# A two-part transformer block in fp32: the MLP's mean squares, the residual's scale and the final norm's root computed in another way

## The chip, the cores and the metric

The kernel runs on one core of one Trainium2 chip. The metric is the time of one execution in device microseconds (us); lower is better. Weights, inputs and the result lie in the chip's HBM.

## What is computed

A sequence of 256 tokens of width 1024 goes through two blocks. The first has two layers, each a mixer (convolution with attention, then a gated linear recurrence) and an MLP of width 4096; the second is an attention block with modulation. Cut to what the change touches:

```python
def rmsnorm(x, g):
    xf = x.astype(jnp.float32)
    y = xf * lax.rsqrt(jnp.mean(xf * xf, axis=-1, keepdims=True) + EPS)
    return (y * g.astype(jnp.float32)).astype(x.dtype)

def first_block(x, ...):
    for layer in range(DEPTH):                     # DEPTH = 2
        h = rmsnorm(x, mix_norm[layer])
        ...
        x = x + y
        x = x + sq_relu_mlp(rmsnorm(x, mlp_norm[layer]), w_up[layer], w_down[layer])
    return rmsnorm(x, final_norm)

def second_block(x, c, ctx, ...):
    ...
    y = (jax.nn.sigmoid(ga) * ya + jax.nn.sigmoid(gb) * yb) @ w_out[i]
    x = x + gate * y
    return rmsnorm_2(x, final_g)                   # the same formula
```

`sq_relu_mlp(h, up, down)` is the square of relu(h @ up), times down. As the square scales with the square of h, the MLP's norm can be put behind it: its output is multiplied by 1 / (mean square + eps), which the code calls R2, with no root.

## The kernel before

**Layout.** Activations stand transposed: 128 channels of a group on the partitions, 8 groups, 256 tokens along the free axis (`x` is 128 x 8 x 256). Every fp32 weight is split into a rounded part and its residue (`wh`, `wl`), every activation too, and one product becomes three on TensorE (`mm3`, lines 358 to 362).

**Weights.** 240 blocks of 128x1024 come in a fixed order through `fetch` (line 300): a DMA on SyncE's queue into one of four `raw` buffers, then ScalarE's copy to `wh` (line 307) and a subtraction to `wl` on VectorE or GpSimd (line 310; the table `POLICY` says which). Six buffers of each kind, ten from the first MLP to the fourth step of the second, hold what is ready; `unit` keeps up to six blocks prepared ahead. A load waits until the residue of the block four earlier has been taken from its buffer, and all loads of SyncE stand in one queue.

**The MLP** (`mlp`, lines 939 to 985). Sixteen steps p: two blocks of `up` give 256 hidden channels (`mm`), ScalarE takes relu and square (lines 955, 956), GpSimd the exact square (957), VectorE the residue (`mal`, line 407). From p = 2 on, two blocks of `down` per step are summed into four PSUM tiles `acc`. The last four rows of `down` and the addition to the residual come in `proj_tail`, which needs R2 (line 835). At p = 4 `ssq` sums the squares of x over the channel groups (ScalarE, GpSimd); at p = 6 `csum` (line 424) sums over the partitions with two products of one column, tokens on the partitions, and VectorE adds eps and takes the reciprocal of 128x2 numbers (`rv`); at p = 8 `spread` turns these back with two products with the identity (line 442) and a ScalarE copy (448) into a 128x256 tile that holds the scale of each token on every partition.

**Beside the first MLP** the modulation of the second block is computed: 12 loads of 1 MB (`mw`, line 880, on SyncE's queue among the weight loads, two buffers) and 40 multiply-and-sum operations on VectorE (`mdump`, line 883), then a few small operations on their sums (`mod`, lines 926 to 935).

**The second block.** `b2_head` computes `r1`, the root of the first block's final norm, two numbers per partition. `b2_kv` makes keys and values, `b2_attn` the attention, `b2_out` the output projection: `oproj` and gates for four pairs p, then eight rows of `w_out` into PSUM. At p = 1 `b2_out` spreads `r1` (line 1461) and multiplies the residual by it (1463). The final norm: for each pair of channel groups b, VectorE adds the gated output to the residual (1492), ScalarE squares it (1493), `fold` adds the two squares of a pair (1484; GpSimd for b below 2, VectorE else); `scale` multiplies by the gain (1481). `stat` (1477) sums over channels with one-column products, five of them; `meaneps` (VectorE, 430), a power -0.5 on GpSimd (`rsq`, 435) and `across` (442) give the scale, with which the five output pieces are multiplied (1511) and stored.

The order of the instructions on each engine is set by a scheduler from the order of the code; `issue_after` holds an instruction back behind a named one.

## Time and profile before

| | us |
|---|---|
| median of three timed runs | 832.42 |
| lowest, highest | 828.91, 835.37 |
| the profiled execution | 829.35 |
| its span, first to last instruction | 827.5 |
| TensorE busy in the span | 790.3 |
| VectorE busy | 589.2 |
| ScalarE busy | 457.4 |
| GpSimd busy | 220.6 |

Engines in rows: PE is TensorE, PEld its weight loads, DVE VectorE, ACT ScalarE, POOL GpSimd, SP SyncE; a q behind a name is the engine's queue, which issues transfers. A row of the timeline has the start, the time until its last instruction ends, engine, line, operation, written tile, read tiles, form and count, and in brackets how long the engine stood idle before it and what ended that. Products on TensorE overlap: their lengths add up to more than the time they take, so the time of a group is read from the starts. An fp32 product that isn't split leaves two records.

### The profile page before, as it was taken

To read this page: it belongs to the slowest core of one execution; us is meant where nothing else is said; L and a number is where in the kernel's file an instruction comes from. 1 tells how busy PE (TensorE), PEld (TensorE's weight loads), DVE (VectorE), ACT (ScalarE), POOL (GpSimd) and SP (SyncE) were. 2 spreads that over 40 slices of the span, in tenths; PEclk is the share of its full clock that TensorE was granted. 3 is DMA by queue.
4 is the path that set the end of the run, shared out by engine and by line. 5 is a ranking of instruction groups with operands and counts; after the bars stand their busy time and mean duration, and the time that the engine had idled before them with its cause. 6 is when DMAs were issued, how large, how long until landed. Compare 5 with 4: busy or idle time off the path is not lost.

```text
span 827.5 us, 16152 instructions
## 1 busy us (share of the span) xinstructions
PE 790.3 (96%) x6476; PEld 757.8 (92%) x6476; DVE 589.2 (71%) x956; ACT 457.4 (55%) x722; POOL 220.6 (27%) x160
## 2 busy tenths in 40 slices
PE   6999899999999978798999999999999999999996
PEld 6997799999999978698999999999989988889996
DVE  6899659999997698898638445557634877566743
ACT  5578546544446625576636444545626587765433
POOL 4886634110111465500441101111000022220001
PEclk9999999999999999799999999999999999999998
DMA  7864357878878744318646566665234532554621
GB/s 237 305 204 128 102 179 240 336 269 301 289 275 280 250 120 136 112 49 303 222 126 202 185 183 201 191 194 177 85 126 142 165 104 101 179 166 166 204 78 51
DMA packets 41259, 152.32 MB, mean 184 GB/s; under 512 B 4576, under 2 KB 5088, under 8 KB 39008
## 3 DMA queue, kind: packets, MB, share of 16 engines
q1 hardware_dynamic: 40752, 149.19, 55.4%
q10 hardware_dynamic: 432, 2.10, 0.6%
q8 instruction: 51, 0.84, 0.4%
q14 instruction: 24, 0.20, 0.1%
HBM read 149.17 MB, written 2.10 MB: 183 GB/s over the span
## 4 chain that ended last, share of the span: by engine, by line
PE 74%; DVE 11%; ACT 5%; DMA 3%; issue 3%; POOL 2%; SPq 0%; POOLq 0%; DVEq 0%; ACTq 0%
PE mm L360 13%; PE mm L361 13%; PE mm L362 12%; PE acc L361 10%; PE acc L360 9%; PE acc L362 9%; DMA raw<-in_wst 3%; PE acc L1320 2%; PE acc L1348 2%; PE mm L1357 2%; DVE wl L310 2%; ACT wh L307 1%; DVE ysl L407 1%; POOL wl L310 1%; PE mm L442 1%
## 5 line engine op out<-in xcount | busy, mean ns | idle before, releaser
L307 ACT ACTIVATE wh<-raw 128x1024 fp32r<-128x1024 f32 (+1 forms) x198 | 207.1, 1049 | 185.6 <-PE mm L361 77.3
L310 DVE TENSOR_TENSOR wl<-raw,wh 128x1024 fp32r<-128x1024 f32 (+1 forms) x167 | 208.8, 1257 | 109.5 <-ACT wh L307 109.4
L361 PE MATMUL mm<-xsl,wh 128*128 128x256 f32 x824 | 229.7, 279 | 1.5 <-DVE xsl L847 1.5
L360 PE MATMUL mm<-xsh,wh 128*128 128x256 f32 x824 | 231.0, 280 | 0.0
L362 PE MATMUL mm<-xsh,wl 128*128 128x256 f32 x824 | 229.6, 279 | 0.0
L360 PEld LDWEIGHTS mm<-xsh,wh 128*128 128x128 f32 x824 | 156.0, 189 | 3.7 <-issue 3.3
L361 PEld LDWEIGHTS mm<-xsl,wh 128*128 128x128 f32 x824 | 156.0, 189 | 2.6 <-DVE xsl L847 2.1
L362 PEld LDWEIGHTS mm<-xsh,wl 128*128 128x128 f32 x824 | 155.6, 189 | 0.0
L957 POOL TENSOR_TENSOR ma<-mr 128x512 f32<-128x512 f32 x32 | 49.7, 1554 | 233.7 <-ACT mr L955 233.7
L361 PE MATMUL acc<-mal,wh 128*128 128x256 f32 x384 | 106.6, 278 | 0.7 <-DVE mal L407 0.7
L360 PE MATMUL acc<-mah,wh 128*128 128x256 f32 x384 | 106.7, 278 | 0.0
L362 PE MATMUL acc<-mah,wl 128*128 128x256 f32 x384 | 106.3, 277 | 0.0
L310 POOL TENSOR_TENSOR wl<-raw,wh 128x1024 fp32r<-128x1024 f32 x36 | 87.9, 2463 | 27.9 <-ACT wh L307 27.2
L361 PEld LDWEIGHTS acc<-mal,wh 128*128 128x128 f32 x384 | 72.4, 188 | 1.3 <-DVE mal L407 1.3
L362 PEld LDWEIGHTS acc<-mah,wl 128*128 128x128 f32 x384 | 72.1, 188 | 0.0
L360 PEld LDWEIGHTS acc<-mah,wh 128*128 128x128 f32 x384 | 72.1, 188 | 0.0
L307 ACT ACTIVATE wxh<-raw 128x1024 fp32r<-128x1024 f32 x35 | 36.6, 1056 | 34.7 <-DMA raw<-in_wst 27.0
L883 DVE CUSTOM_DVE_ANT_0 mdump<-mw,cv 128x1024 f32<-128x1024 f32 x40 | 51.0, 1274 | 3.4 <-DMA mw<-in_modw 3.1
L310 DVE TENSOR_TENSOR wxl<-raw,wxh 128x1024 fp32r<-128x1024 f32 x34 | 43.7, 1305 | 9.4 <-ACT wxh L307 9.4
L361 PE MATMUL mm<-xsl,wxh 128*128 128x256 f32 x168 | 47.5, 283 | 1.9 <-DVE xsl L847 1.9
L360 PE MATMUL mm<-xsh,wxh 128*128 128x256 f32 x168 | 47.6, 284 | 0.2 <-ACT xsh L841 0.2
L362 PE MATMUL mm<-xsh,wxl 128*128 128x256 f32 x168 | 47.2, 281 | 0.0
(374 smaller groups left out, 1765.1 us busy)
## 6 DMA issues: line engine op xcount, KB each, us to landing
raw<-in_wst SPq DMA_DIRECT2D x240, 512.0 KB, 4.1
mw<-in_modw SPq DMA_DIRECT2D x12, 1024.0 KB, 7.5
nb<-in_nab SPq DMA_DIRECT2D x16, 256.0 KB, 3.6
ab<-in_alibi ACTq DMA_DIRECT2D x1, 1536.0 KB, 7.8
x<-in_xT SPq DMA_DIRECT2D x4, 256.0 KB, 5.2
cv<-in_cvec SPq DMA_DIRECT2D x1, 1024.0 KB, 4.7
cx<-in_cT SPq DMA_DIRECT2D x1, 1024.0 KB, 6.5
xd<-x SPq DMA_DIRECT2D x1, 1024.0 KB, 4.4
```

Source lines behind the costliest of these rows:

```text
L307: nc.scalar.activation(wh, r, AF.Copy)
L310: (nc.vector if lo == "v" else nc.gpsimd).tensor_tensor(wl, r, wh.bitcast(F32), op=ALU.subtract)
L360: mm(out, w[0], x[0], start=start, stop=False, skip_group_check=True)
L361: mm(out, w[0], x[1], start=False, stop=False, skip_group_check=True)
L362: return mm(out, w[1], x[0], start=False, stop=stop, skip_group_check=True)
L407: self.nc.vector.tensor_tensor(l, src, h.bitcast(F32), op=ALU.subtract)
L442: self.lasts = self.nc.tensor.matmul(ps[:, j * 128:(j + 1) * 128], rc[:, j:j + 1].to_broadcast([128, 128]), self.ident, start=True, stop=True)
L883: V.tensor_tensor_reduce(d, w, cv[:, s * 1024:(s + 1) * 1024], 0.5, 0.0, op0=ALU.mult, op1=ALU.add, accum_out=self.mod[:, s * 24 + i:s * 2 ...
L957: G.tensor_tensor(a, r, r, op=ALU.mult)
L1320: PE.matmul(sc[i], Q[tag, h][a][:, qs], K[tag, h][b], start=a + b == 0, stop=a == 1)
L1348: PE.transpose(pt[:, i * 128:(i + 1) * 128], P[:, i * 128:(i + 1) * 128], self.ident)
L1357: PE.matmul(o[64 * hh:64 * hh + 64, :T], vt[:, i, h * 64:h * 64 + 64], PTs[tag, h][:, i], start=i == 0, stop=i == 3, skip_group_check=True)
```

## The change

In the MLP, at p = 6, one product takes the place of the two of `csum`: the 128x256 tile of squares is the moving operand and a 128x128 tile of ones the fixed one, so that the sum over partitions comes out on every partition at once, as a 128x256 tile. VectorE multiplies, adds eps and takes the reciprocal of all 256 columns. The spread at p = 8 is gone. A pad of 32 bytes in layer 0 stands where `rv` stood, so that later tiles keep their addresses. `r1` is spread at the end of `b2_kv` into the pool of the second block (its later tiles move by 1024 bytes), not in `b2_out`. In the final norm the folds of b = 0 and 1 are added on GpSimd, so that there are four statistics, not five; the root is taken by ScalarE, the reciprocal by VectorE; ScalarE's table for roots is loaded behind the last tanh; the scalings of b = 2 and 3 come behind the root.

```diff
@@ -968,11 +968,13 @@
             if p == 4:
                 parts = self.ssq(mp, x)
             if p == 6:
-                v = self.meaneps(self.csum(parts), D)
-                rv = self.t(self.cp, [128, 2], "rv")
-                V.reciprocal(rv, v)
-            if p == 8:
-                R2 = self.spread(mp, rv, "R2")
+                if l == 0:
+                    self.pad(self.cp, 32)
+                ms = self.ps()[:, :T]
+                PE.matmul(ms, self.ones, parts[0], start=True, stop=True)
+                R2 = self.t(mp, [128, T], "R2")
+                V.tensor_scalar(R2, ms, 1.0 / D, EPS, op0=ALU.mult, op1=ALU.add)
+                V.reciprocal(R2, R2)
             if p >= 2:
                 for k in (2 * p - 4, 2 * p - 3):
                     self.krow(acc, self.unit("down"), A.pop(k), k == 0, False)
@@ -1257,6 +1259,7 @@
                 V.scalar_tensor_tensor(cf[:, k], cf[:, k], self.p("gcq", k), RQ, op0=ALU.mult, op1=ALU.mult)
                 self.split(cf[:, k], cq[0][:, k], cq[1][:, k])
         zpair("za", 1, ep, cqn)
+        d["R1"] = self.spread(bp, d["r1"], "R1")
         d.update(kb=kb, vb=vb, krh=krh, krl=krl, ck=ck, wk=wk, va=va, bp=bp)
         q8 = self.t(self.cp, [128, 8, T], "hch")
         for i in range(2):
@@ -1389,7 +1392,7 @@
         def gdone(nm, p):
             def f(ps):
                 tg[nm, p] = self.t(bp, [128, 512], f"t{nm}", bufs=2)
-                S.activation(tg[nm, p], ps, AF.Tanh, scale=0.5)
+                self.lastt = S.activation(tg[nm, p], ps, AF.Tanh, scale=0.5)
             return f
 
         def gpair(nm, p):
@@ -1458,14 +1461,17 @@
             V.tensor_tensor(y, y, tg["gb", p], op=ALU.add)
             self.split(self.pair(y), ys[0][:, 2 * p:2 * p + 2], ys[1][:, 2 * p:2 * p + 2])
             if p == 1:
-                R1 = self.spread(op, d["r1"], "R1")
                 for k in range(8):
-                    V.scalar_tensor_tensor(x[:, k], x[:, k], self.p("fin", k), R1, op0=ALU.mult, op1=ALU.mult)
+                    V.scalar_tensor_tensor(x[:, k], x[:, k], self.p("fin", k), d["R1"], op0=ALU.mult, op1=ALU.mult)
         def orow(w, k, ms, end):
             for m in ms:
                 o = last[:, :T] if m == 7 else acc[m // 2][:, (m % 2) * T:(m % 2 + 1) * T]
                 c = slice(m * 128, m * 128 + 128)
                 self.mm3(o, (w[0][:, c], w[1][:, c]), yrow(k), k == 0 and (m % 2 == 0 or m == 7), end)
+        eps = self.t(op, [128, 1], "eps")
+        G.memset(eps, EPS)
+        with self.tc.issue_after(self.lastt.ins):
+            S.activation(self.warm, self.warm, AF.Sqrt)
         for k in range(6):
             orow(self.unit("wo2"), k, range(8), False)
         ws = [self.unit("wo2") for _ in range(2)]
@@ -1478,7 +1484,8 @@
                           stop=end, skip_group_check=True)
         def scale(b):
             for k in (2 * b, 2 * b + 1):
-                S.activation(x[:, k], x[:, k], AF.Copy, scale=self.p("fg2", k))
+                i = S.activation(x[:, k], x[:, k], AF.Copy, scale=self.p("fg2", k))
+            return i
 
         def fold(b):
             (G if b < 2 else V).tensor_tensor(sq[b][:, 0], sq[b][:, 0], sq[b][:, 1], op=ALU.add)
@@ -1498,14 +1505,20 @@
         with self.tc.issue_after(xi.ins):
             fold(2)
         with self.tc.issue_after(si.ins):
-            for b in range(1, 4):
-                scale(b)
+            sc = scale(1)
+        G.tensor_tensor(sq[0][:, 0], sq[0][:, 0], sq[1][:, 0], op=ALU.add)
         stat(sq[0][:, 0], True)
-        stat(sq[1][:, 0])
         stat(sq[3][:, 0])
         stat(sq[2][:, 0])
         stat(sq[3][:, 1], end=True)
-        RF = self.across(self.rsq(self.meaneps(st[:, :2], D)))
+        sd = self.t(op, [128, 2], "sd")
+        with self.tc.issue_after(sc.ins):
+            sd_ = S.activation(sd, st[:, :2], AF.Sqrt, scale=1.0 / D, bias=eps)
+        with self.tc.issue_after(sd_.ins):
+            scale(2)
+            scale(3)
+        V.reciprocal(sd, sd)
+        RF = self.across(sd)
         for i, (k0, k1) in enumerate(((0, 1), (1, 3), (3, 5), (5, 7), (7, 8))):
             xb = x[:, k0:k1]
             V.tensor_tensor(xb, xb, self.b2(RF, k1 - k0), op=ALU.mult)
```

What moves in the order. SyncE's queue in the first MLP, where `raw` are weight loads and `mw` modulation loads, before:

```order
L300 DMA raw_2814<-in_wst 128x1024
L880 DMA mw_3328<-in_modw 128x2048
L300 DMA raw_2846<-in_wst 128x1024
L300 DMA raw_2879<-in_wst 128x1024
L880 DMA mw_3402<-in_modw 128x2048
L300 DMA raw_2909<-in_wst 128x1024
L300 DMA raw_2951<-in_wst 128x1024
L880 DMA mw_3507<-in_modw 128x2048
L300 DMA raw_2983<-in_wst 128x1024
L300 DMA raw_3016<-in_wst 128x1024
L300 DMA raw_3048<-in_wst 128x1024
```

and now:

```order
L300 DMA raw_2808<-in_wst 128x1024
L300 DMA raw_2840<-in_wst 128x1024
L880 DMA mw_3322<-in_modw 128x2048
L300 DMA raw_2873<-in_wst 128x1024
L300 DMA raw_2903<-in_wst 128x1024
L880 DMA mw_3396<-in_modw 128x2048
L300 DMA raw_2945<-in_wst 128x1024
L300 DMA raw_2977<-in_wst 128x1024
L300 DMA raw_3010<-in_wst 128x1024
L880 DMA mw_3501<-in_modw 128x2048
L300 DMA raw_3042<-in_wst 128x1024
```

The numbers in the names differ by a few between the two programs (raw_2951 is now raw_2945); the last `mw` stands behind raw_3010, which was raw_3016, two weight loads further back, and the one before it one load further back.

VectorE in the same place, where `mdump` reads a modulation load, `wl` and `wxl` are weight residues and `mal` that of an MLP pair, before:

```order
L883 ISA mdump_3509,mod_1436<-mw_3507,cv_1433 128x1024
L883 ISA mod_1436 128x1
L310 TENSOR_TENSOR wxl_2954<-raw_2951,wxh_2953 128x1024
L883 ISA mdump_3541,mod_1436<-mw_3507,cv_1433 128x1024
L883 ISA mod_1436 128x1
L926 TENSOR_TENSOR mod_1436<-mod_1436,par_70 128x24
L932 SCALAR_TENSOR_TENSOR Ax_3726<-mod_1436,par_70 128x8
L935 TENSOR_SCALAR gate_3728<-mod_1436 128x8
L933 TENSOR_TENSOR Ax_3726<-Ax_3726,par_70 128x8
L310 TENSOR_TENSOR wxl_2986<-raw_2983,wxh_2985 128x1024
L310 TENSOR_TENSOR wxl_3019<-raw_3016,wxh_3018 128x1024
L310 TENSOR_TENSOR wxl_3051<-raw_3048,wxh_3050 128x1024
```

and now:

```order
L883 ISA mdump_3503,mod_1436<-mw_3501,cv_1433 128x1024
L883 ISA mod_1436 128x1
L310 TENSOR_TENSOR wxl_2980<-raw_2977,wxh_2979 128x1024
L883 ISA mdump_3535,mod_1436<-mw_3501,cv_1433 128x1024
L883 ISA mod_1436 128x1
L310 TENSOR_TENSOR wxl_3013<-raw_3010,wxh_3012 128x1024
L926 TENSOR_TENSOR mod_1436<-mod_1436,par_70 128x24
L932 SCALAR_TENSOR_TENSOR Ax_3720<-mod_1436,par_70 128x8
L935 TENSOR_SCALAR gate_3722<-mod_1436 128x8
L933 TENSOR_TENSOR Ax_3720<-Ax_3720,par_70 128x8
L310 TENSOR_TENSOR wxl_3045<-raw_3042,wxh_3044 128x1024
L407 TENSOR_TENSOR mal_2940<-ma_2938,mah_2939 128x512
```

Two weight residues that stood behind the small operations on the sums (wxl_2986 and wxl_3019, now 2980 and 3013) stand ahead of them, one between the two reductions and one behind the second; the residue that stood between the reductions is ahead of both.

TensorE at the end of the program, where csq_1503 to csq_1506 (now 1499 to 1502) are the squares of the four pairs, before:

```order
L362 MATMUL mm_9158<-kb_9152,wl_9781 128x256
L1477 MATMUL mm_9808<-ones_83,csq_1503_9809 128x1 x2
L1477 MATMUL mm_9808<-ones_83,csq_1504_9810 128x1 x2
L1477 MATMUL mm_9808<-ones_83,csq_1506_9812 128x1 x2
L1477 MATMUL mm_9808<-ones_83,csq_1505_9811 128x1 x2
L1477 MATMUL mm_9808<-ones_83,csq_1506_9812 128x1 x2
L442 MATMUL mm_9902<-ident_78,rc_9900 128x128 x2
```

and now:

```order
L362 MATMUL mm_9150<-kb_9144,wl_9771 128x256
L1483 MATMUL mm_9798<-ones_83,csq_1499_9799 128x1 x2
L1483 MATMUL mm_9798<-ones_83,csq_1502_9802 128x1 x2
L1483 MATMUL mm_9798<-ones_83,csq_1501_9801 128x1 x2
L1483 MATMUL mm_9798<-ones_83,csq_1502_9802 128x1 x2
L442 MATMUL mm_9890<-ident_78,sd_9883 128x128 x2
```

One statistic is gone, and what is spread is VectorE's `sd`, no longer GpSimd's `rc`; the first statistic reads a tile that GpSimd's added operation writes.

## Rows read from the trace of the kernel before

**Rows 1.** The page, busy time, share of the span and instructions of engines.

```profile
PE 790.3 (96%) x6476; PEld 757.8 (92%) x6476; DVE 589.2 (71%) x956; ACT 457.4 (55%) x722; POOL 220.6 (27%) x160
```

**Rows 2.** Windows: length, PE, PEld, DVE, ACT, POOL busy (instructions), clock, DMA, GB/s.

```profile
185.00:200.00 15.00, 15.00 (x131) 15.00 (x130) 14.93 (x22) 6.07 (x8) 3.07 (x2) 1.00 0.89 296
284.00:310.00 26.00, 20.85 (x177) 20.05 (x175) 23.11 (x27) 7.56 (x14) 15.48 (x9) 1.00 0.45 132
...
480.00:560.00 80.00, 80.00 (x708) 80.00 (x708) 41.14 (x38) 38.22 (x44) 11.18 (x7) 1.00 0.63 195
...
640.00:660.00 20.00, 19.97 (x160) 18.92 (x159) 17.51 (x29) 10.62 (x16) 0.71 (x1) 1.00 0.55 175
```

**Rows 3.** Timeline of TensorE: a layer-0 statistic, and that of the first MLP.

```profile
89.08 0.70 PE L780 MATMUL mm<-conv,on 128*128 128x256 f32 x2 [0.24 <-DVE conv L581]
89.62 0.72 PE L424 MATMUL mm<-ones,conv 128*128 128x1 f32 x6
...
175.46 0.50 PE L424 MATMUL mm<-ones,ssum 128*128 128x1 f32 x4
...
176.02 0.28 PE L361 MATMUL acc<-mal,wh 128*128 128x256 f32 x1
```

**Rows 4.** Timeline of TensorE at the spread in the output stage.

```profile
760.40 0.60 PE L442 MATMUL mm<-ident,r 128*128 128x128 f32 x4
...
760.96 0.28 PE L361 MATMUL mm<-xsl,wh 128*128 128x256 f32 x1
```

**Rows 5.** VectorE: the small reciprocal (timeline), and a 128x256 form (shortest/median/longest, ns).

```profile
189.59 0.15 DVE L973 RECIPROCAL rv<-var 128x2 f32<-128x2 f32 x1
...
L625 DVE TENSOR_TENSOR qk<-mm,R x4: 415/415/416, 41.6 to 60.9; 128x256 f32<-128x256 f32 x4
```

**Rows 6.** Timeline of VectorE and SyncE's queue at the last modulation loads.

```profile
227.26 1.22 DVE L883 CUSTOM_DVE_ANT_0 mdump<-mw,cv 128x1024 f32<-128x1024 f32 x1 [1.74 <-DMA mw<-in_modw]
...
233.92 1.23 DVE L883 CUSTOM_DVE_ANT_0 mdump<-mw,cv 128x1024 f32<-128x1024 f32 x1 [1.39 <-DMA mw<-in_modw]
...
241.23 1.22 DVE L883 CUSTOM_DVE_ANT_0 mdump<-mw,cv 128x1024 f32<-128x1024 f32 x1
...
232.93 0.42 SPq L880 DMA_DIRECT2D mw<-in_modw  x1
236.32 3.44 SPq L300 DMA_DIRECT2D raw<-in_wst  x2
```

**Rows 7.** Timeline of GpSimd, VectorE, TensorE at the end of the first MLP.

```profile
277.87 2.75 POOL L310 TENSOR_TENSOR wl<-raw,wh 128x1024 fp32r<-128x1024 f32 x1 [0.60 <-ACT wh L307]
...
281.65 0.69 DVE L407 TENSOR_TENSOR mal<-ma,mah 128x512 fp32r<-128x512 f32 x1 [3.30 <-POOL ma L957]
...
282.39 0.39 PE L361 MATMUL acc<-mal,wh 128*128 128x256 f32 x1 [0.19 <-DVE mal L407]
```

**Rows 8.** Timeline of GpSimd, TensorE and VectorE in the tail.

```profile
816.37 0.74 POOL L1484 TENSOR_TENSOR csq<-csq 128x256 f32<-128x256 f32 x1 [0.36 <-ACT csq L1493]
...
817.38 2.29 PE L1477 MATMUL mm<-ones,csq 128*128 128x1 f32 x20
...
817.98 0.42 DVE L1484 TENSOR_TENSOR csq<-csq 128x256 f32<-128x256 f32 x1
...
819.71 0.16 DVE L430 TENSOR_SCALAR var<-mm 128x2 f32<-128x2 f32 x1 [1.31 <-PE mm L1477]
...
819.95 0.71 POOL L435 TENSOR_TENSOR rc<-var,mhalf 128x2 f32<-128x2 f32 x1 [2.85 <-DVE var L430]
...
820.71 0.71 PE L442 MATMUL mm<-ident,rc 128*128 128x128 f32 x4 [1.04 <-POOL rc L435]
```

**Rows 9.** Groups, ScalarE: a small activation; busy us, mean ns, idle before.

```profile
L468 ACT ACTIVATE warm<-warm 128x1 f32<-128x1 f32 x1 | 0.2, 203 | 0.0
```

**Rows 10.** Windows in layer 1, columns as in rows 2.

```profile
336.00:340.00 4.00, 0.00 (x0) 0.00 (x0) 4.00 (x3) 0.00 (x0) 4.00 (x2) 0.72 0.50 189
...
344.00:348.00 4.00, 4.00 (x21) 4.00 (x20) 2.48 (x7) 3.28 (x8) 0.00 (x0) 0.50 0.36 123
```

## The prediction

> **What bounds the kernel now.** I read the page's engine shares first, then the busy time by stage, then what TensorE waited for, and only then the timeline around each edited place. TensorE is busy 96% of the span [rows 1]. By stage: in the first MLP (131 products in 15.00 us, busy 15.00) and in the second (708 in 80.00) it never stops; where the first MLP hands over to layer 1 (284 to 310 us) it is busy 20.85 of 26.00 us [rows 2]. So an edit inside an MLP or the second block is worth the TensorE time that it takes off, as long as nothing else sets the end of that stage, and at the very end of the program, where one dependent step follows another, it is worth the latency of the step.
>
> The sum is made on the profiled execution: 829.35 us, of which 827.5 are the span and 1.85 lie around it. The median of the three timed runs is 832.42, 3.07 above it, and these runs lie 6.46 apart; I put the difference worked out below on the median. About 1% (8 us) is what a measurement of this kernel can tell from no change.
>
> **MLP mean squares, TensorE.** Before, two products with one column, four records, start at 175.46, and the second product of the next group starts at 176.02. Ordinary products follow each other by 0.12, so one of them would have started 0.12 after 175.46: the four records cost 0.56 - 0.12 = 0.44 us [rows 3]. The spread of the two columns (four records again, 128 columns each) is priced at the same form in the output stage: 760.40 to 760.96, less 0.12, again 0.44 [rows 4]. Both go: 0.88 in each MLP. One fp32 product with 256 columns comes in. The nearest row is the layer-0 pair of records of that form, 89.08 to 89.62, 0.54, after a wait; as four records of half as many columns cost 0.44, two of 256 columns should cost the same. I take 0.44, bounds 0.44 and 0.54. Net -0.44 in each MLP (-0.34 at the other end).
>
> **MLP mean squares, VectorE and ScalarE.** Out go a 128x2 multiply-add of 0.16 [rows 8], a 128x2 reciprocal of 0.15 [rows 5] and, on ScalarE, one 128x256 copy, which no stop of TensorE hangs on. In come a 128x256 multiply-add out of PSUM and a 128x256 reciprocal. The first is priced at the 128x256 product out of PSUM, 0.42 [rows 5]. No row has a wide reciprocal: the two-column one shows only fixed cost. [...] I take 0.42, since the 128x2 reciprocal lasts no longer than the multiply-add of that size. [...] In the second MLP it is covered: TensorE is full there and VectorE has half its time free (41.14 busy of 80.00) [rows 2]. In the first MLP VectorE is full too (14.93 of 15.00) [rows 2]; there the cover is the two stops in which it waits for modulation weights, 1.74 and 1.39 us [rows 6], 3.1 together.
>
> [...]
>
> **The first MLP's queue.** The order shows what the edit moves: on SyncE each of the last six modulation loads now stands behind one more weight load, the last behind two more. A wait is thereby added in front of them: the loads stand behind weight loads that wait for VectorE to free a raw buffer. Before, the last one issued at 232.93, and the next weight load at 236.32 [rows 6]. The reduction that needs it started at 241.23, 8.3 after the issue [rows 6]; behind it on VectorE stand a second reduction, the small operations on the sums, four weight residues and the residue of an MLP pair, and SyncE's next weight loads wait for those. VectorE now does the weight residues earlier and the reductions later, so those weight loads wait less. I take the last landing 0.8 later; bounds -0.5 (the residues come so early that the load does too) and +2.0.
>
> Does that reach TensorE? It does at one place: the stage's last pair. GpSimd's weight residue at 277.87 takes 2.75, the square of the last pair comes behind it, its residue on VectorE starts at 281.65, and TensorE stops 0.19 for it at 282.39 [rows 7]. That chain hangs on weight loads and buffers, not on TensorE. So the 0.44 that TensorE gains is spent waiting there, and what the chain moves is what counts. Some of the 0.8 is caught up in the 30 us between, where VectorE has gaps; I take +0.4, with bounds -0.44 (all follows TensorE) and +2.0.
>
> **The second MLP.** No such wait: TensorE is full from 480 to 560 [rows 2]. -0.44 stays.
>
> **The scale a stage sooner.** The same four records of 0.44 move from the output stage [rows 4] to the end of the key/value stage. TensorE is full there too (19.97 of 20.00), ScalarE gets one short copy more where it is busy half the time (10.62 of 20.00) [rows 2]. Net 0; +0.44 if the old place had been covered, -0.44 if the new one is. The eight VectorE multiplications that use it keep their place. The rows of ScalarE and VectorE that change order in the attention swap with one neighbour; no TensorE wait there hangs on them.
>
> **The tail.** Before, 20 one-column records run from 817.38 without a gap, 2.29 in all, and VectorE's multiply-add starts at 819.71; then 0.16, a hop of 0.08, GpSimd's power 0.71, a hop of 0.05, and TensorE spreads at 820.71: 1.00 from statistic to spread [rows 8].
>
> After: one block fewer, 16 records, at 2.29 / 20 = 0.114 each 1.83. But the first now needs GpSimd's new addition. The fold before it starts at 816.37 and lasts 0.74, to 817.11; another 0.74 and a hop give 817.93 [rows 8], 0.55 after 817.38. The last record ends at 819.76, where it was 819.67: +0.09. So the four dropped records are not a gain; GpSimd takes their place. Then ScalarE's root 0.20 (the nearest row, a 128x1 activation) [rows 9], a hop 0.08, the reciprocal 0.15, a hop 0.05: 0.48 in place of 0.96. I count 0.09 - 0.48 = -0.39; if the root costs twice its row, -0.2; if GpSimd's addition were covered, -0.85. Four of ScalarE's scalings now stand behind the root; the first two of the five output products need none of them, and I cost them at nothing; one output product late by one scaling is inside the bounds. The table load that comes behind the last tanh lies beside TensorE's remaining products, for which the weights are converted up to six blocks ahead: 0.
>
> [...]
>
> **Sum.** First MLP +0.40, second -0.44, scale 0, tail -0.39: -0.43. On its own execution 828.9; on the median 832.0.
>
> **Rivals.**
> - All gains kept: the chain before 282 follows TensorE. -0.44 - 0.44 - 0.39 = -1.27, so 831.1. For it: the wait was only 0.19. Against it: the chain shown runs through loads and GpSimd.
> - Slower through the queue: the modulation loads land late and their reductions hold up the weight residues behind them on VectorE, so the residue of the last pair is 2.0 later. Price +2.0; it decides from the point where the shift passes the 0.83 won later. +2.0 - 0.83 = +1.17, so 833.6. For it: VectorE already stood twice for such loads [rows 6], and the stage's end has no slack [rows 7]. [...]
> [...]
>
> **How the numbers follow.** Forecast 0.45, all kept 0.22, slower queue 0.18, eight passes 0.15. No case comes near 8 us, so same 0.94; what is left, 0.03 each way, is for the hand-over to layer 1, where the stops of TensorE are of several us and could fall otherwise. The cases and their bounds reach from 830.3 (all kept, GpSimd's addition and the moved spread covered) to 835.6; the runs of before lie 3.5 below and 3.0 above their median, and a median of few runs keeps part of that. So 828.4 to 835.8.
>
> **What would show it.** In the MLPs: one product line in place of two, TensorE short by 0.44, VectorE's 128x256 reciprocal at 0.4 (right) or over 2 us. At the end of the first MLP a wait for the last pair's residue of 0.6 to 1.5 us in place of 0.19. In the tail the first statistic starting near 817.9 (on the old scale) behind GpSimd, and 0.5 us from last record to spread. Wrong if that wait is gone, if a new one shows in the attention, or if the time leaves the range.

## The result and the profile after

The changed kernel takes 836.90 us, median of 20 runs (832.92 to 838.93), against 831.77 for the kernel before (20 runs, 825.92 to 838.06): ratio 1.0058, 95% interval 1.0035 to 1.0080. That is within 1%, as forecast, but on the slower side, and the time lies above the predicted range. Ratios in this document are estimates from the runs of both kernels, not quotients of the two medians; each set of experiments was timed beside runs of its own of the kernel before (medians 830.23 to 832.55).

The profiled execution is 833.72 us long, its span 831.9 against 827.5. The page of after, the answer to [rows 1], has TensorE busy longer and with fewer instructions:

```profile
PE 794.4 (95%) x6460; PEld 761.5 (92%) x6460; DVE 590.1 (71%) x956; ACT 458.2 (55%) x723; POOL 220.6 (27%) x161
```

Where the 4.4 us arise is read from TensorE's timeline at places that both kernels have: the MLP's statistic, the next stage's first statistic, twice over, and the last spread. After:

```profile
176.11 0.59 PE L974 MATMUL mm<-ssum,ones 128*128 128x256 f32 x2
...
306.01 0.49 PE L424 MATMUL mm<-ones,s 128*128 128x1 f32 x3 [1.25 <-POOL s L861]
...
453.12 0.59 PE L974 MATMUL mm<-ssum,ones 128*128 128x256 f32 x2
...
580.17 0.28 PE L424 MATMUL mm<-ones,s 128*128 128x1 f32 x2
...
825.16 0.68 PE L442 MATMUL mm<-ident,sd 128*128 128x128 f32 x4 [0.70 <-DVE sd L1520]
```

Before, the first of these is in [rows 3] (175.46), the last in [rows 8] (820.71), and the others are:

```profile
302.32 0.38 PE L424 MATMUL mm<-ones,s 128*128 128x1 f32 x2 [0.65 <-POOL s L861]
...
449.86 0.39 PE L424 MATMUL mm<-ones,ssum 128*128 128x1 f32 x3
...
573.84 0.28 PE L424 MATMUL mm<-ones,s 128*128 128x1 f32 x2
```

| from | to | before | after | difference |
|---|---|---|---|---|
| start | first MLP's statistic | 175.46 | 176.11 | +0.65 |
| first MLP's statistic | layer 1's first statistic | 126.9 | 129.9 | +3.0 |
| layer 1's first statistic | second MLP's statistic | 147.5 | 147.1 | -0.4 |
| second MLP's statistic | second block's first statistic | 124.0 | 127.0 | +3.0 |
| that statistic | last spread | 246.9 | 245.0 | -1.9 |
| last spread | end of the span | 6.8 | 6.8 | 0.0 |

The first row is within the scatter: no part of the change stands there, and that stretch took 174.7 to 178.9 us over the 20 profiles of this document. The loss is in the two MLPs, 3 us each, where unsplit products had been saved. No wait explains it: from the first MLP's statistic to the next stage's, TensorE waited 2.3 us before (1.5 for the split of the next stage's input, 0.6 for the statistic's sum, 0.2 for the last pair) and 2.7 after, and the wait for the last pair [rows 7] is gone. TensorE's waits after, 175 to 307 us (what waited for what: us in all, times, longest):

```profile
PE mm L361 <- DVE xsl L847: 1.4, 1, 1.4
PE mm L424 <- POOL s L861: 1.3, 1, 1.3
```

What differs is how many products TensorE gets through in a stretch that it fills. Windows of after, columns as in [rows 2]:

```profile
205.00:280.00 75.00, 75.00 (x639) 75.00 (x638) 62.48 (x77) 39.58 (x46) 12.48 (x8) 1.00 0.83 280
480.00:560.00 80.00, 80.00 (x681) 80.00 (x681) 39.86 (x37) 37.62 (x43) 11.15 (x7) 1.00 0.61 188
780.00:815.00 35.00, 35.00 (x311) 35.00 (x310) 18.55 (x20) 15.67 (x18) 0.00 (x0) 1.00 0.47 149
```

The same windows of before (480 to 560 us: 708 products, in [rows 2]):

```profile
205.00:280.00 75.00, 75.00 (x664) 75.00 (x663) 61.59 (x73) 40.53 (x48) 15.48 (x9) 1.00 0.82 279
...
780.00:815.00 35.00, 35.00 (x299) 35.00 (x299) 14.66 (x17) 11.28 (x15) 0.00 (x0) 1.00 0.23 78
```

TensorE is busy all the time in all of them and the granted clock is 1.00. Yet the MLP windows hold 639 and 681 products instead of 664 and 708, and the one of the output projection 311 instead of 299. From start to start, the products of 256 columns follow each other in one of two pitches. In the second MLP of after, from 453.67 to 572.15, 1006 steps take 118.48 us, 117.8 ns each (long pitch); in before, from 473.60 to 565.74, 813 steps take 92.14 us, 113.3 ns each (short pitch). The difference is 4.45 ns a product. Either pitch lasts for hundreds of products. In the MLPs from the statistic on, and in the output projection from its spread on, it turns with no wait ahead only where an unsplit fp32 product (statistic or spread) stands between; elsewhere it also turns behind a single step of 0.20 us that shows as no wait (756.44 to 756.64 before: 117.5 ns ahead of it, 113.8 behind), and where the granted clock comes back from 0.50 to 1.00, near 109.1 us before, steps of 213 ns become steps of 113. Before, in each MLP: long behind the statistic for 190 products, short behind the spread of step 8 for the rest. After: long behind the wide product, and no spread comes to end it. Counted over the whole profile, 1559 steps have the long pitch before and 2777 after: 1218 x 4.45 ns = 5.4 us. Less the 0.44 saved in each MLP this is 4.5; the spans differ by 4.4.

### The profile page after: what moved, and what is told of

The parts are those of the page before. It is cut to its first block, busy times and chain, and to the rows that moved or that the text cites. A ratio compares the mean times of both kernels' runs of the same rounds, so it can differ in the third digit from the quotient of the medians.

```text
span 831.9 us, 16120 instructions
## 1 busy us (share of the span) xinstructions
PE 794.4 (95%) x6460; PEld 761.5 (92%) x6460; DVE 590.1 (71%) x956; ACT 458.2 (55%) x723; POOL 220.6 (27%) x161
## 4 chain that ended last, share of the span: by engine, by line
PE 73%; DVE 11%; ACT 5%; DMA 4%; issue 4%; POOL 3%; SPq 0%; POOLq 0%; DVEq 0%; ACTq 0%
PE mm L360 12%; PE mm L361 12%; PE mm L362 12%; PE acc L361 10%; PE acc L362 10%; PE acc L360 10%; DMA raw<-in_wst 2%; PE acc L1323 2%; PE acc L1351 2%; PE mm L1360 2%; DVE mm L581 1%; DMA cx<-in_cT 1%; DVE ysl L407 1%; POOL wl L310 1%; DVE wl L310 1%
## 5 line engine op out<-in xcount | busy, mean ns | idle before, releaser
L310 DVE TENSOR_TENSOR wl<-raw,wh 128x1024 fp32r<-128x1024 f32 (+1 forms) x167 | 206.3, 1243 | 106.7 <-ACT wh L307 106.0
```

Source lines behind the costliest of these rows:

```text
L310: (nc.vector if lo == "v" else nc.gpsimd).tensor_tensor(wl, r, wh.bitcast(F32), op=ALU.subtract)
```

## The experiments

The expectations call the short pitch fast and the long one slow. Each kernel has one profile; the pitch with which a stage begins differs from execution to execution (244 products ahead of every edit have 117.8 ns in before, from 17.88 us, and 113.4 in after, from 18.72), so a ratio mixes several courses and a profile shows one. The profiles of e6, e7 and e17 are the slowest runs of their kernels. As the stretch ahead of the first MLP's statistic alone scatters by 4.3 us, profiles are compared here stage by stage.

**The three parts, each alone (e1 to e3).** e1: the diff of the MLP alone; e2: `R1` spread a stage sooner alone; e3: the tail alone.

```
e2
         zpair("za", 1, ep, cqn)
+        d["R1"] = self.spread(bp, d["r1"], "R1")
...
-                R1 = self.spread(op, d["r1"], "R1")
```

> The kernel before with the MLP part of the change alone. Pitch theory (in a full stretch TensorE's split products start every 113.3 or every 117.8 ns, and an unsplit fp32 product between them decides which): before, the statistic set the slow pitch and the spread two steps later set the fast one again; now the wide product sets the slow one and nothing sets it back, so the 730 products after the first spread and the 813 after the second are slow: 1543 x 4.45 ns = +6.9, less 2 x 0.44 of TensorE time saved: +6.0 us against before, and rows with a pitch of 117.8 from the wide product to the end of both MLPs. Queue theory (the modulation loads and VectorE's longer rows hold the first MLP up): +1 to +3, with waits of TensorE in the first MLP and an unchanged pitch in the second.

> The kernel before with the early spread of the residual's scale alone. Pitch theory: the spread in the output stage set the slow pitch for the 478 products behind it; without it they stay fast, -478 x 4.45 ns = -2.1 us; the few products between the new place and the attention turn slow, +0.3: -1.8 in all. Queue theory and my prediction: 0.

> The kernel before with the tail of the change alone: one statistic fewer, GpSimd's added fold, ScalarE's root. All theories: -0.2 to -0.5 us, TensorE waiting 0.6 for GpSimd before the first statistic and about 0.7 before the last spread instead of 1.04.

Measured: e1 839.44 us, ratio 1.0077 (1.0046 to 1.0109). e2 828.15, 0.9960 (0.9936 to 0.9983). e3 832.10, 0.9995 (0.9973 to 1.0017). The MLP part alone makes the loss and more; the early spread, forecast at nothing, is the gain; the tail cannot be told from nothing. In e2 the output projection has the short pitch (312 products), the MLPs are as before:

```profile
205.00:280.00 75.00, 75.00 (x664) 75.00 (x663) 60.31 (x73) 41.38 (x48) 16.82 (x10) 1.00 0.84 285
480.00:560.00 80.00, 80.00 (x708) 80.00 (x707) 41.12 (x38) 38.20 (x45) 11.19 (x7) 1.00 0.62 196
780.00:815.00 35.00, 35.00 (x312) 35.00 (x311) 15.55 (x20) 12.69 (x18) 1.11 (x2) 1.00 0.27 82
```

**What turns the pitch back (e4 to e7).** To the change is added, behind the wide product: e4 a spread product of a constant that nobody reads, at step 8, where before has its spread; e5 only the PSUM buffer that the spread would take; e6 the unread spread directly behind the wide product; e7 a pair of one-column products at step 8, also unread.

```
e4             if p == 8:
+                  self.across(self.mhalf)
e5             if p == 8:
+                  V.memset(self.ps()[:, 0:1], 0.0)
e6                 PE.matmul(ms, self.ones, parts[0], start=True, stop=True)
+                  self.across(self.mhalf)
e7             if p == 8:
+                  self.csum([parts[0]])
```

> The changed kernel with one more pair of products in each MLP, of the form of the old spread and in its old place (step 8), on a constant, its result read by nobody. Pitch theory: the pair sets the fast pitch again; 730 + 813 products are fast: -6.9 + 0.9 = -6.0 against the changed kernel, that is about 831 beside 837, 1 us below before. Queue theory: the pair only costs, +0.9 against the changed kernel.

> The changed kernel in which step 8 of each MLP takes a PSUM buffer as the old spread did, and VectorE sets one column of it; no product is added, and the buffers of all later products are those of the kernel before. Bank theory (the slow pitch comes from the PSUM buffers that the later products and their readers share since one buffer less is taken): the fast pitch is back behind step 8, -6 us against the changed kernel. Pitch theory (the kind of product in between decides, not the buffer): no change, 837, slow to the end of both MLPs.

> The changed kernel with a pair of the spread's form on a constant directly behind the wide product, at step 6. Pitch theory: the pair sets the fast pitch at once, so the 189 products between steps 6 and 8 of each MLP are fast too: -6.0 - 1.7 = -7.7 us against the changed kernel, about 829, some 2.5 below before. If only the first of two adjacent groups counts, it stays slow, +0.9.

> The changed kernel with a pair of the old statistic's form (one column each, four records, as many as the spread) at step 8, its result read by nobody. Pitch theory, if the form decides (in both traces the one-column pair left the slow pitch behind it, also where it was slow already): stays slow, +0.9 against the changed kernel. If any such group flips the pitch, whatever its form: -6.0.

Measured: e4 835.03, ratio 1.0029 (1.0006 to 1.0052); e5 835.67, 1.0048 (1.0026 to 1.0070); e6 832.06, 1.0008 (0.9987 to 1.0029); e7 836.24, 1.0057 (1.0036 to 1.0079). The taken buffer does nothing (682 products from 480 to 560 us), nor does the one-column pair (682). e4 was a miss: in its profile the spread at step 8 left the long pitch long in both MLPs (682). In e6 the second MLP is short throughout: 1006 steps at 113.35 ns and 123.1 us in place of 127.0. So the pitch is the second MLP's loss. The first MLP is short in e6 too, but takes 132.5 us: there TensorE now waits. Windows, then the waits from 176 to 312 us:

```profile
480.00:560.00 80.00, 80.00 (x709) 80.00 (x707) 39.93 (x38) 40.34 (x46) 12.80 (x8) 1.00 0.60 193
```

```profile
PE acc L361 <- DVE mal L407: 3.9, 3, 2.7
PE mm L361 <- DVE xsl L847: 1.5, 1, 1.5
PE mm L424 <- POOL s L861: 1.2, 1, 1.2
```

**Two spreads, and a spread from the short pitch (e8, e14).** Before, with the unread spread behind the spread of step 8 (e8), and behind the statistic of step 6 (e14).

```
e8                 R2 = self.spread(mp, rv, "R2")
+                  self.across(self.mhalf)
e14                v = self.meaneps(self.csum(parts), D)
+                  self.across(self.mhalf)
```

> The kernel before with one more pair of the spread's form directly behind the spread of step 8. Pitch theory, if each spread flips the pitch: slow, fast, slow again, and 1543 products turn slow: +6.9 + 0.9 = +7.8 us against before. If a spread always leaves the fast pitch: +0.9. Queue theory: +0.9.

> The kernel before with an unread spread right behind the statistic at step 6 of each MLP. If a spread turns the pitch over (slow to fast, and fast to slow as the residual's spread in the output stage): 190 products fast behind the pair, and then 839 and 814 slow behind the spread of step 8, (1653 - 379) x 4.45 ns = +5.7 us and 0.9 us for the two spreads, ratio 1.008. If a spread leaves the fast pitch whatever stood before it: 379 products fast instead of slow, -1.7 + 0.9 = -0.8 us, ratio 0.999.

Measured: e8 831.56, ratio 0.9998 (0.9977 to 1.0019): short behind the two spreads, as if there were one. e14 835.05, 1.0031 (1.0011 to 1.0051). In its profile the 190 products behind statistic and spread are short, and the spread of step 8, which before turns long to short, now turns short to long, in both MLPs (second MLP 127.1 us). The sign is that of "turns over"; by the profile (3011 long steps, span 832.4 against 827.5) three quarters of the size, by the timed runs under half of it.

```profile
205.00:280.00 75.00, 75.00 (x639) 75.00 (x638) 61.18 (x74) 40.36 (x47) 15.16 (x9) 1.00 0.83 282
480.00:560.00 80.00, 80.00 (x682) 80.00 (x681) 38.99 (x35) 38.04 (x43) 11.15 (x7) 1.00 0.59 185
```

**The width (e10, e11).** The wide product cut into two of 128 columns, the spread's width: in the change (e10), and in the MLP part alone (e11).

```
-                PE.matmul(ms, self.ones, parts[0], start=True, stop=True)
+                for h in range(2):
+                    PE.matmul(ms[:, 128 * h:128 * h + 128], self.ones,
+                              parts[0][:, 128 * h:128 * h + 128], start=True, stop=True)
```

> The change with the wide product of the MLP's mean squares cut into two products of 128 columns, the width of the spread's. Theory A, that the width of the last unsplit product sets the pitch behind it: the stretches behind it run at 113.33 ns in both MLPs, which takes 1218 x 4.45 ns = 5.4 us and 379 x 4.45 ns = 1.7 us off the slow products of the change and of before, so 2 to 4 us faster than before, ratio 0.995 to 0.998. Theory B, that a product over all rows with the ones as weights or moving data leaves the slow pitch whatever its width, and only the spread's identity product the fast one: as the change, ratio 1.004 to 1.008.

> The MLP part alone, with its wide product cut into two of 128 columns; all else as before. Theory A (width): both MLPs at 113.33 ns, 379 products x 4.45 ns = 1.7 us and the 0.44 us per MLP of the dropped products less than before, about -2 us, ratio 0.997. Theory B (ones): as the MLP part with the wide product, which measured 1.0077.

Measured: e10 835.55, ratio 1.0052 (1.0022 to 1.0082); e11 837.08, 1.0086 (1.0054 to 1.0119). The width does not decide: three of the four stretches behind the halves are long. The fourth (first MLP of e11) came in with the long pitch and left with the short one, which speaks against "ones leave it long" as well. The other three came in short, so in all four places the halves turned the pitch over.

**Versions without the first MLP's edit (e9, e15).** e9: the change without the MLP part. e15: the change with the first MLP as before, and in the second the wide product with an unread spread directly behind it.

```
e15
+            if p == 6 and l == 0:
                 v = self.meaneps(self.csum(parts), D)
...
+            if p == 6 and l == 1:
                 PE.matmul(ms, self.ones, parts[0], start=True, stop=True)
+                self.across(self.mhalf)
```

> The change without its MLP part: the residual's scale spread a stage sooner and the tail of the change, the MLP of before. If the pitch of TensorE's split products is the cause, the MLPs stay as before (189 or 190 products at 117.78 ns behind each statistic, then over 800 at 113.33) and the 478 products of the output projection run at 113.33: -2.1 us from these, -0.4 from the tail, so about 2.5 us faster than before, ratio 0.997. The rival, that the early spread or the tail has a cost of its own that only shows beside the MLP part, gives a ratio over 1.000.

> The change with the first MLP as before, and in the second MLP an unread spread right behind the wide product. By the pitch: second MLP fast all through, -0.8 us; output projection fast, -2.1 us; tail -0.4 us; in all -3.3 us, ratio 0.996. If what the change without its MLP part showed (0.9999) is the rule and the early spread brings nothing beside the new tail: 0.999.

Measured: e9 830.23, ratio 0.9999 (0.9979 to 1.0020), a miss, though its profile has the forecast pitch: the MLPs are as before, and the stretch from the second block's first statistic to the last spread takes 244.8 us (246.9 before). Why its runs don't show the gain stays open. e15 828.95, 0.9973 (0.9946 to 1.0000), short of 0.996. In e15's profile the second MLP is short (123.4 us), but the output projection long (300 products in 35 us), though its spread stands early. Over all 20 profiles the output projection is short in 9 of the 12 with the early spread and in 1 of the 8 with the late one. So the early spread makes the short pitch likelier; it does not ensure it.

**The first MLP (e12, e13, e16 to e18).** Does VectorE's wide reciprocal make the last pairs late? e12 and e16 add it to before, into a tile that nobody reads (e16 takes the mean square as scale, so that it runs later). e13, e17 and e18 are e6 without it in both MLPs, in the first, in the second; there the MLP is multiplied by the mean square instead of by its inverse.

```
e12                V.reciprocal(rv, v)
+                  RX = self.t(mp, [128, T], "RX")
+                  V.tensor_scalar(RX, parts[0], 1.0 / D, EPS, op0=ALU.mult, op1=ALU.add)
+                  V.reciprocal(RX, RX)
e16
+                  V.tensor_scalar(RX, parts[0], v[:, 0:1], EPS, op0=ALU.mult, op1=ALU.add)
e17            V.tensor_scalar(R2, ms, 1.0 / D, EPS, op0=ALU.mult, op1=ALU.add)
-              V.reciprocal(R2, R2)
+              if l == 1:
+                  V.reciprocal(R2, R2)
```

> The kernel before with VectorE's two wide instructions of the change added at step 6 of each MLP (scale and reciprocal over 128x256, on the square sums themselves, into a tile that nobody reads); TensorE's products stay as before. Theory 'VectorE makes the last pair late': the pair that TensorE waits for at 282 us comes about 1.5 to 2.2 us later, from the statistic at 175 us to the next one at 302 us the first MLP takes 128.3 to 129 us instead of 126.8, the second MLP the same as before: ratio 1.002. Theory 'the pitch alone': no change, 126.8 us and ratio 1.000.

> The change with an unread spread right behind the wide product (as in the run that had the fast pitch in both MLPs) and without the wide reciprocal: the MLP's result is multiplied by the mean square instead of by its inverse. Theory 'VectorE makes the last pair late': the first MLP, 132.5 us with the reciprocal, comes to 127 us or under, and the whole to a ratio of about 0.996. Theory that the lateness has nothing to do with the reciprocal: 131 to 133 us there and a ratio of 1.000.

> As the kernel before with two wide VectorE instructions added (into a tile that nobody reads), but made to depend on the mean square, so that they run near 190 us, where the change has its wide reciprocal, and not at 125 us as in the first form of this run. Theory 'the wide reciprocal in the crowded stretch makes the last pair late': the first MLP, from statistic to statistic, 128.5 us or more (126.8 in before, 126.4 to 127.4 in five other profiles with its products), TensorE waiting 1.5 us or more for the last pair of VectorE; ratio 1.002. Theory that it has cover: 126 to 127.5 us, ratio 1.000.

> The change with the unread spread behind the wide product, and the wide reciprocal in the second MLP alone (the first MLP's result is multiplied by the mean square). Theory 'wide reciprocal': first MLP 125.5 to 127 us with the fast pitch, second MLP 123 us. Theory that the first MLP's time is a matter of when the weights come: anything from 126 to 133 us.

> The same with the wide reciprocal in the first MLP alone (the second MLP's result is multiplied by the mean square). Theory 'wide reciprocal': first MLP 130 to 133 us with the fast pitch and TensorE waiting 2.5 us or more for VectorE's last pairs, second MLP 123 us. Theory that the first MLP's time is a matter of when the weights come: anything from 126 to 133 us.

Measured: e12 833.96, ratio 1.0018 (0.9996 to 1.0041); e13 830.41, 0.9996 (0.9966 to 1.0026); e16 833.29, 1.0011 (0.9984 to 1.0039); e17 827.31, 0.9950 (0.9921 to 0.9979); e18 832.34, 0.9993 (0.9961 to 1.0025). The time of e13 missed its 0.996, and the first MLP of e17 came out long where short was expected. Both MLPs of every profile, from statistic to statistic, in us:

| kernel | first | second | kernel | first | second |
|---|---|---|---|---|---|
| before | 126.9 | 124.0 | e9 | 126.4 | 124.0 |
| after | 129.9 | 127.0 | e10 | 133.9 | 127.1 |
| e1 | 132.8 | 127.0 | e11 | 130.2 | 127.3 |
| e2 | 127.2 | 124.0 | e12 | 127.2 | 124.0 |
| e3 | 127.2 | 124.2 | e13 | 126.1 | 123.1 |
| e4 | 130.3 | 127.5 | e14 | 129.4 | 127.1 |
| e5 | 130.5 | 127.3 | e15 | 129.1 | 123.4 |
| e6 | 132.5 | 123.1 | e16 | 131.0 | 124.0 |
| e7 | 132.4 | 127.5 | e17 | 130.3 | 123.1 |
| e8 | 127.4 | 124.7 | e18 | 126.1 | 123.1 |

The second MLP falls into three groups without overlap, by its pitch alone: long throughout (127.0 to 127.5), long for 190 products and then short (124.0 to 124.7), short throughout (123.1 to 123.4). The wide reciprocal does not show there (without it in e13 and e18, with it in e6 and e17: all 123.1).

The first MLP has no such order. With the long pitch behind the statistic or the spread of step 8 it took 129.4 to 133.9 us (after, e1, e4, e5, e7, e10, e14, e17); with the short one 126.1 to 127.4 in eight profiles, but 129.1 to 132.5 in four (e6, e11, e15, e16).

Two pairs of profiles part the pitch from the rest, since up to the next stage's statistic each engine has the same instructions in the same order in both. In e13 and e17 (taken on two chips) TensorE's pitch is short and long, with no wait for a last pair in either: the first MLP takes 126.1 and 130.3 us. So the pitch is the larger part of the first MLP's loss too. Windows of e13 and, second, of e17:

```profile
205.00:280.00 75.00, 75.00 (x664) 75.00 (x663) 62.01 (x75) 42.66 (x48) 16.25 (x9) 1.00 0.84 290
205.00:280.00 75.00, 75.00 (x640) 75.00 (x639) 61.55 (x74) 38.26 (x43) 13.62 (x8) 1.00 0.81 282
```

In e6 and e18 (two chips again) both first MLPs have the short pitch and the wide reciprocal, yet they take 132.5 and 126.1 us. So the late last pair comes and goes between executions of the same instructions. What the four late profiles share is a late modulation load: VectorE's last reduction of one starts 68.9 to 72.5 us behind the statistic, in the eight others 65.2 to 68.1. That is the way of the prediction's queue rival, but no run moves the loads alone. The last reduction in e6 (statistic at 177.88) and, second, in e18 (178.94):

```profile
250.08 1.23 DVE L883 CUSTOM_DVE_ANT_0 mdump<-mw,cv 128x1024 f32<-128x1024 f32 x1
245.66 1.22 DVE L883 CUSTOM_DVE_ANT_0 mdump<-mw,cv 128x1024 f32<-128x1024 f32 x1
```

e16 agrees with the reciprocal's being the cause (131.0 us, a wait of 2.0 for VectorE's last pair), e18 does not (126.1 with the reciprocal at 193 us, no such wait), and e15 is late without any wide reciprocal. e12 ran its reciprocal at 125 us, ahead of the crowded stretch, and so did not test it. So the reciprocal is not shown to be the cause, and what makes the first MLP late in those four stays open. The waits of e16 and, second, of e18, from 176 to 312 us (the first of e18 lies behind the next stage's statistic):

```profile
PE acc L361 <- DVE mal L407: 2.0, 1, 2.0
PE mm L361 <- DVE xsl L847: 1.5, 1, 1.5
PE mm L424 <- POOL s L861: 1.3, 1, 1.3
```

```profile
PE mm L442 <- POOL rc L435: 2.2, 1, 2.2
PE mm L361 <- DVE xsl L847: 1.6, 1, 1.6
PE mm L424 <- POOL s L861: 1.2, 1, 1.2
```

## Why the prediction was wrong

The step that failed is "Net -0.44 in each MLP". It priced the products by the time of their own records, as if those behind were untouched. The records do cost what was forecast: the wide pair runs from 176.11 to 176.65, 0.54 with one split product in it, so 0.43. But the pair that went out, the spread, had also turned the pitch of some 840 and 814 products behind it from long to short, and the sum put that at nothing. Some 1650 products x 4.45 ns are +7.4 us, less the 0.88 saved +6.5; the two MLPs measured +3.0 each.

- **Second MLP, -0.44 forecast:** +3.0 measured. 813 more products at the long pitch are +3.6, which leaves -0.6 for the products saved: that term had about the right size. With the pitch kept short behind the wide product the stage takes 123.1 us (e6, e13, e17, e18), -0.9 against before. There one more spread has taken back the saving, and 190 products x 4.45 ns = 0.85 us account for the rest.
- **First MLP, +0.40 forecast:** +3.0 measured. The mechanism named, that TensorE would wait longer for the last pair's residue, did not come, and the prediction had named a vanished wait as a sign of being wrong: VectorE now waits for TensorE behind it (1.60 us; 0.48 before):

```profile
283.55 0.69 DVE L407 TENSOR_TENSOR mal<-ma,mah 128x512 fp32r<-128x512 f32 x1 [3.31 <-POOL ma L957]
284.15 1.22 DVE L310 TENSOR_TENSOR wxl<-raw,wxh 128x1024 fp32r<-128x1024 f32 x1
286.98 0.70 DVE L835 TENSOR_TENSOR acc<-acc,R 128x512 f32<-128x512 f32 x1 [1.60 <-PE acc L362]
```

  That this stage's end has two bounds, TensorE and VectorE's last pair, was right: in e6 and e16 the pair ends it. The modulation loads did come later, by more than the 0.8 forecast: the last issue at 237.58 (before 232.93), VectorE waiting 3.10 us for a load at 245.56.
- **The scale a stage sooner, 0 forecast:** the place from which the spread went has the gain. At 760.40 [rows 4] it turned short to long for the 478 products of the output projection; without it they run short: 478 x 4.45 ns = 2.1 us, beside the -1.9 of the table's fifth row. e2 alone measured -0.4% (0.9960).
- **The tail, -0.39 forecast:** about nothing. From the start of the last product to the spread it takes 3.56 us (821.60 to 825.16) where it took 3.45 (817.26 to 820.71). Three terms were off, by 0.50 in all: GpSimd's addition holds up the first record by 0.79 and not 0.55 (0.64 of it shows as a wait); 16 records take 1.95 instead of 1.83; and the wait behind them fell by 0.34, from 1.04 [rows 8] to 0.70, and not by 0.48 (the root takes 0.26, not 0.20). GpSimd's addition (821.74 to 822.46) and VectorE's fold (822.31 to 822.74) overlap in the profile, and the fold takes 0.43 where it took 0.42, so it is not seen to be held up, though the profile's times of GpSimd are rough.

```profile
821.60 0.28 PE L362 MATMUL mm<-kb,wl 128*128 128x256 f32 x1
822.51 1.95 PE L1483 MATMUL mm<-ones,csq 128*128 128x1 f32 x16 [0.64 <-POOL csq L1509]
```

- **The reciprocal, 0.42 forecast:** 1.74 us, in both MLPs, four times the forecast: beyond the 0.15 of the 128x2 form [rows 5] it costs (1.74 - 0.15) / (0.42 - 0.15) = 5.9 times as much as the product that it was priced at. The eight passes among the chances, and the "over 2 us" that goes with them, were an assumption of the author's that no run shows; the runs showed 1.74. TensorE did not wait for it, nor for anything else from 190 to 200 us and from 450 to 475.

```profile
L977 DVE RECIPROCAL R<-R x2: 1737/1742/1746, 191.9 to 457.1; 128x256 f32<-128x256 f32 x2
```

- **The rivals.** "Slower through the queue" had the sign but not the place: half of the loss is in the second MLP, where nothing waits. What it describes, a last pair over 2 us late, shows in e6 (a wait of 2.7). The 2 us for layer 1 in the upper end of the cases, 835.6, are shown by no run: the granted clock there was 0.50 from 342 to 348 us in after and from 338 to 347.5 in before, and the stage took 147.1 us against 147.5. The chance of 0.94 for "within 1%" held by luck: none of its cases had the pitch, which happens to be worth 5.4 us here, 0.65%.

## What to carry to other kernels

In this kernel an unsplit product among hundreds that follow back to back was worth its own time (0.43 us for the wide one) and what it did to the pitch of those behind it (3.6 us for 813 of them in the second MLP). So, ahead of an edit that takes out, moves or adds an unsplit product, compare products per microsecond in full windows at the same granted clock on both sides of it in the profile of before: if the counts differ by 4%, the stretch behind it (products x 4.45 ns here) is the larger term. The profile of before had the sign: 708 products in 80 us of the second MLP are 8.85 per us, 299 in 35 us behind the spread of the output projection 8.54. Of the versions that compute the right result the one that measured best is the smallest, the early spread alone (e2, ratio 0.9960, 0.9936 to 0.9983); that its gain holds with the new tail is not shown (e9, 0.9999).

## What the runs showed of the hardware

TensorE full, at a granted clock of 1.00, showed two pitches for these 256-column products: 113.3 ns (813 steps in the second MLP of before) and 117.8 ns (1006 in that of after). What a product did to the pitch, at all places of the 20 profiles with no wait and products of one pitch on both sides:

| between the products | short to long | long to short | stays long | stays short |
|---|---|---|---|---|
| one-column pair (sums of squares) | 44 | 0 | 13 | 0 |
| spread of a computed scale | 25 | 70 | 0 | 0 |
| wide product | 10 | 0 | 0 | 0 |
| its two halves | 3 | 1 | 0 | 0 |
| wide product, unread spread directly behind | 0 | 2 | 1 | 6 |
| one-column pair, unread spread directly behind | 0 | 0 | 0 | 2 |
| spread, unread spread directly behind | 0 | 2 | 0 | 0 |
| unread spread 190 products behind the wide one | 0 | 0 | 2 | 0 |

A spread of a computed scale turned the pitch over each time, 95 of 95; a one-column pair left it long each time, 57 of 57. The wide product met the short pitch in all ten places, so the table does not tell whether it sets the long pitch or turns over whatever it meets. The unread spreads do not fit one rule (the last row against the fifth). The pitch that comes in does not decide either: behind the wide product and an unread spread the long pitch turned short in the first MLPs of e13 and e18 and stayed long in that of e17. So what the pitch hangs on inside TensorE stays open. Behind a wait either pitch occurs: behind TensorE's wait of 0.43 us for VectorE's `xsl` in layer 1, 118 steps take 113.5 ns each in before (from 391.69 us) and 117.8 in after (from 392.77). That this makes part of the scatter of one kernel's runs is likely but was not measured.
